# A hybrid SSM and attention layer: the row of reciprocal softmax sums is stored by one transfer from ScalarE's queue, and put in order by its load

## The chip, the cores and the metric

The kernel runs on one core of a Trainium2 chip. The metric is device time in microseconds, the median of several runs; beside it stands one execution taken by the hardware profiler, from which all durations and waits come. The engines are TensorE (PE, with its weight loads PEld), VectorE (DVE), ScalarE (ACT), GpSimd (POOL) and SyncE (SP), which here only issues transfers. Transfers are issued by SyncE, ScalarE and GpSimd, each from its own in-order queue, and carried by 16 DMA engines.

## The reference, cut to what matters

The layer normalises x, multiplies it by one wide matrix, and feeds two branches, a Mamba-2 scan and a forgetting attention, that are gated, merged, multiplied by an output matrix and added to x. The change lies in the attention. There are 16 heads of 64 channels, a sequence of 1024, and queries in 8 blocks of 128:

```
s = einsum(q, k) * scale + fcum[query] - fcum[key]
s = where(key <= query, s, -inf)
prob = softmax(s)
o = einsum(prob, v)
y_att = o * silu(z_att)
```

All numbers are float32. Where precision needs it, an operand is split in a high and a low part.

## The kernel before

**Stages.** The projections are matrix products by a seven-product scheme on halves of the operands (classes `Pair` and `Plain`), 12 matrix multiplications of 128x512 for each product. They form one long stream (`Stream`), and everything else is done beside it: first the scan (to about 600 us), then attention (about 660 to 1146 us), then the rest of the branch and output products. Attention calls `fill`, which lets the stream run for so many half products between two pieces of attention, and so gives TensorE work while VectorE and ScalarE deal with the scores. The operands of the later branch products (tiles x0 to x6, an h and an l part each) are loaded and split during the second half of attention, from about 930 us on.

**Attention.** The loop at L1666 goes over 8 pairs of heads (hp), and for each over six groups g of two query blocks against half of the keys. In a step, `scores` makes the products q k in a PSUM bank s (4 such banks, also used for pt and tp below). VectorE adds the forget bias fb and takes the extreme (L1526, tile nm), ScalarE takes the exponential and its sum (L1530, tile sm). `turned` transposes the result with TensorE (pt), and copies it out (p, L1548 on VectorE, L1550 on ScalarE). `weighted` multiplies by v into a bank av.

**The row of reciprocal sums.** After every second group, three times for a pair of heads (n = 0, 1, 2), the sums are brought together (`settle`, `scale`), which gives a tile ns of 128 queries x 8 columns: two parts h, two heads e of the pair, two query blocks t. The output has channels on the partitions and queries along the row, so the values must lie along a row, the same on all 64 partitions of a head. `send` turns ns with TensorE (tp), ScalarE copies the 8x128 result to st (L1452), and GpSimd stores it with two transfers (L1454) to st_dram, with the order changed so that a head's 512 values follow each other. `take` loads that row for each head e by SyncE to 64 partitions of rb (L1460). VectorE multiplies av by the gate (`free`, L1479), and later by rb (`out`, L1491 for n < 2, L1485 for n = 2). The first pair's three rows are stored near 689, 711 and 730 us, and the last pair's last one near 1136 us: 24 rows in all.

**What sets the order.** A scheduler orders each engine's instructions, except that TensorE's, and all that are wrapped in `pin`, keep the order of the program. The two stores L1454 are pinned. GpSimd does little else in attention: differences of operands (L214, L1587, L1593, L1607) and their stores (L196), stores of outputs (ya_dram, L1581) and of gated branch products (ms_dram, L1102). ScalarE's queue issues the stores of gates gs and ga (L654), 256 KB each, right behind the tanh that makes them (L653). ScalarE also makes the high parts of weights (wop, L354), copies of PSUM (s, L410 and L418) and of operands (L278, L281). SyncE issues all loads and some stores, in order: while it waits for a store to land before a load, the loads behind it wait too. Transfers from SyncE and ScalarE share eight semaphores, used in turn; one that takes a semaphore waits until the earlier transfer on it has landed.

Of the kernel before, what the change touches and what calls it, by code (L numbers as in the profile page):

```python
# [8 lines left out]
F32 = mybir.dt.float32  # L9
# [7 lines left out]
P = 128  # L17
T = 1024
D = 1024
NK = D // P  # L20
KH = NK // 2
NT = T // P
HALF = 512
# [63 lines left out]
def hybrid_layer(ctx: ExitStack, tc, a, out):  # L87

    nc = tc.nc
# [17 lines left out]
    nc.vector.memset(eps4, 4.0 * EPS)  # L107

    f_dram = tc.dram_tile([HEADS, T], F32, name="f_dram")
    st_dram = tc.dram_tile([NK, 3, 2, HALF], F32, name="st_dram")  # L110
    r_dram = tc.dram_tile([NG, T], F32, name="r_dram")
    rr_dram = tc.dram_tile([NG, T], F32, name="rr_dram")
    cs_dram = tc.dram_tile([HEADS, T], F32, name="cs_dram")
# [18 lines left out]
    def turn(out_, in_, idn=ident):  # L132
        return tc.keep_in_program_order(nc.tensor.transpose(out_, in_, idn))  # L133

    def pin(op):
        return tc.keep_in_program_order(op)

    def small(name="th"):
        return gp.tile([P, HALF], F32, tag="th", name=name)
# [1053 lines left out]
    with tc.tile_pool(name="pro", bufs=1, reuse_waits="tile", side="right") as pro, tc.tile_pool(  # L1193
        name="prop", bufs=1, space=PSUM, reuse_waits="tile", side="right"
# [116 lines left out]
    with tc.tile_pool(name="ssm", bufs=1, reuse_waits="tile", side="right") as sp, tc.tile_pool(  # L1311
        name="ssmp", bufs=1, space=PSUM, reuse_waits="tile", side="right"
# [42 lines left out]
    with tc.tile_pool(name="att", bufs=1, reuse_waits="tile", side="right") as ap, tc.tile_pool(  # L1355
        name="attp", bufs=1, space=PSUM, reuse_waits="tile", side="right"
    ) as pp:
        rows = [slice(64 * e, 64 * e + 64) for e in range(2)]
# [42 lines left out]
        class Heads:  # L1401
# [44 lines left out]
            def send(self, n):  # L1446

                tp = pp.tile([P, HALF], F32, tag="s", bufs=4, name="tp")
                turn(tp[0:8, 0:P], self.ns[n].rearrange("p h e t -> p (h e t)"))
                st = small("st")[0:8, 0:P]  # L1450
                with tc.high_priority():
                    nc.scalar.activation(st, tp[0:8, 0:P], AF.Copy)  # L1452
                for h in range(2):
                    pin(nc.gpsimd.dma_start(st_dram[self.hp, n, :, 256 * h : 256 * h + 256], st[4 * h : 4 * h + 4, :]))  # L1454

            def take(self, n):

                rb = self.rb[n] = small("rb")
                for e in range(2):
                    nc.sync.dma_start(rb[rows[e], :], st_dram[self.hp, n, e : e + 1, :].to_broadcast([64, HALF]))  # L1460

            def load_gates(self, n):

# [300 lines left out]
```

## Time and profile before

| what | value |
|---|---|
| runs (us) | 1291.77, 1297.5, 1297.4 |
| median (us) | 1297.4 |
| profiled execution, its time (us) | 1294.79 |
| profiled execution, its span (us) | 1293.1 |
| mean granted TensorE clock | 0.997 |
| instructions | 21078 |
| HBM traffic over the span | 182 GB/s |
| stores L1454 | 48, 2 KB each |
| loads L1460 | 48, 128 KB each |

The span is the time from the first to the last instruction of the program in the profiled execution; its time as a run is 1.7 us more. In the rows, a tile's buffer numbers are left out, L12 is line 12 of the kernel, SPq and ACTq are the queues' own instructions (an issue of a transfer, a wait), and "out<-in" names what is written and read. A wait is put down to the last of the things waited for. The time from issue to landing is given by tile and source line, for those transfers whose landing the trace shows.

### The profile page before, as it was taken

Reading aid. Unit: us, or ns where it says so; the run is one execution under the profiler, and the core shown is the slowest. Engines: PE = TensorE matmul, PEld = TensorE weight load, DVE = VectorE, ACT = ScalarE, POOL = GpSimd, SP = SyncE. Lnnn points to the kernel's source line nnn. Section 1 sums busy time; section 2 is a strip of 40 time slices with the busy share of each in tenths; the row PEclk is TensorE's granted clock in tenths of the full one; section 3 lists DMA queues with packets and bytes.
Section 4 is the critical chain, followed back from the end, with each engine's and each line's share of the span. In section 5 each row is a group of like instructions: output and inputs, shape, how many; then the busy total and the mean of one; then the engine's idle time right before and its main releaser. Section 6 shows DMA issues by size and latency. Waiting matters only on the chain. (4 is left out here: it accounts for less than half of the span.)

```text
span 1293.1 us, 21078 instructions
## 1 busy us (share of the span) xinstructions
PE 1253.8 (97%) x7066; PEld 986.1 (76%) x7066; DVE 1014.7 (78%) x1979; ACT 794.3 (61%) x1728; POOL 284.6 (22%) x307
## 2 busy tenths in 40 slices
PE   6999999999999999899999999999999999999998
PEld 4787888788888888688776777777767777678786
DVE  6998888888789878788676766676789767876875
ACT  8755666466556756566555666566677556743654
POOL 0000330024102320143001222222121313256052
PEclk9999999999999999999999999999999999999999
DMA  7332543644363545445564657666677657665932
GB/s 281 104 106 71 154 148 121 199 140 146 127 210 116 153 153 164 122 154 154 168 237 153 221 175 224 193 208 196 228 282 250 219 178 253 230 219 189 364 112 102
DMA packets 154669, 233.60 MB, mean 181 GB/s; under 512 B 17216, under 2 KB 62656, under 8 KB 154560
## 3 DMA queue, kind: packets, MB, share of 16 engines
q1 hardware_dynamic: 142016, 205.53, 49.8%
q0 software_dynamic: 6400, 16.10, 3.3%
q10 hardware_dynamic: 6144, 10.62, 2.2%
q8 instruction: 56, 0.92, 0.3%
q14 instruction: 53, 0.43, 0.1%
HBM read 162.99 MB, written 72.34 MB: 182 GB/s over the span
## 5 line engine op out<-in xcount | busy, mean ns | idle before, releaser
L356 DVE TENSOR_TENSOR wop<-sum,wop 128x512 fp32r<-128x512 f32 x174 | 140.5, 808 | 53.4 <-ACT wop L354 52.7
L354 ACT ACTIVATE wop<-sum 128x512 fp32r<-128x512 f32 x174 | 108.8, 626 | 99.0 <-DVE sum L363 44.7
L1530 ACT ACTIVATE ex<-ex,nm 128x512 f32<-128x512 f32 (+1 forms) x192 | 116.1, 606 | 76.9 <-DVE nm L1526 75.7
L410 ACT ACTIVATE s<-pb 128x512 f32<-128x512 f32 x141 | 83.5, 592 | 97.3 <-PE pb L130 95.9
L130 PE MATMUL pc<-x3h,wop 128*128 128x512 f32 x384 | 131.6, 399 | 2.5 <-ACT wop L354 2.0
L130 PE MATMUL pb<-x0h,wop 128*128 128x512 f32 x384 | 132.2, 400 | 0.7 <-ACT x0h L1246 0.6
L130 PE MATMUL pc<-x2h,wop 128*128 128x512 f32 x384 | 131.4, 399 | 0.4 <-DVE u L422 0.4
L130 PE MATMUL pb<-x6h,wop 128*128 128x512 f32 x376 | 129.2, 399 | 1.6 <-ACT s L410 1.6
L130 PE MATMUL pb<-x5h,wop 128*128 128x512 f32 x376 | 128.3, 398 | 1.3 <-ACT s L410 1.3
L130 PE MATMUL pb<-x4h,wop 128*128 128x512 f32 x376 | 128.6, 398 | 0.2 <-DVE wop L356 0.2
L356 DVE TENSOR_TENSOR wop<-raw,wop 128x512 fp32r<-128x512 f32 x149 | 104.3, 702 | 29.8 <-ACT wop L354 29.5
L1526 DVE CUSTOM_DVE_ANT_0 ex<-s,fb 128x512 f32<-128x512 f32 (+1 forms) x192 | 96.8, 553 | 24.4 <-PE s L130 24.3
L354 ACT ACTIVATE wop<-raw 128x512 fp32r<-128x512 f32 x151 | 93.8, 623 | 15.8 <-PE pc L130 10.1
L130 PE MATMUL pd<-x1h,wop 128*128 128x512 f32 x264 | 89.1, 396 | 0.0
L130 PEld LDWEIGHTS pc<-x3h,wop 128*128 128x128 f32 x384 | 72.1, 188 | 20.2 <-issue 3.8
L130 PEld LDWEIGHTS pb<-x0h,wop 128*128 128x128 f32 x384 | 72.5, 189 | 17.2 <-ACT x0h L1246 1.3
L130 PEld LDWEIGHTS pc<-x2h,wop 128*128 128x128 f32 x384 | 72.1, 188 | 16.1 <-DVE u L422 0.8
L130 PEld LDWEIGHTS pb<-x6h,wop 128*128 128x128 f32 x376 | 70.6, 188 | 18.1 <-ACT s L410 2.7
L130 PEld LDWEIGHTS pb<-x5h,wop 128*128 128x128 f32 x376 | 70.6, 188 | 17.5 <-ACT s L410 2.2
L130 PEld LDWEIGHTS pb<-x4h,wop 128*128 128x128 f32 x376 | 70.5, 188 | 15.7 <-issue 0.7
L130 PE MATMUL s<-k,q 64*128 64x512 f32 (+3 forms) x576 | 75.7, 373 | 6.2 <-DVE p L1548 4.4
L214 POOL TENSOR_TENSOR wd<-wd 128x256 f32<-128x256 f32 x32 | 31.3, 978 | 228.3 <-DMA wd<-in_wo 125.7
(341 smaller groups left out, 3012.1 us busy)
## 6 DMA issues: line engine op xcount, KB each, us to landing
raw<-in_wu SPq DMA_DIRECT2D x128, 256.0 KB, 3.7
csb<-cs_dram SPq DMA_DIRECT2D x32, 256.0 KB, 5.5
fb<-f_dram SPq DMA_DIRECT2D x16, 512.0 KB, 6.5
rb<-st_dram SPq DMA_DIRECT2D x48, 128.0 KB, 3.2
wd<-in_wo SPq DMA_DIRECT2D x40, 128.0 KB, 3.1
xt<-in_x SPq DMA_DIRECT2D x8, 512.0 KB, 5.8
gs_dram<-th ACTq DMA_DIRECT2D x16, 256.0 KB, 3.4
qh_dram<-th SPq DMA_DIRECT2D x16, 256.0 KB, 5.2
```

The costliest lines, as they stand in the source:

```text
L130: return tc.keep_in_program_order(nc.tensor.matmul(*args, **kw))
L214: pin(nc.gpsimd.tensor_tensor(t[out_], t[a_], t[b_], ALU.subtract))
L354: nc.scalar.activation(op[:, 0], src, AF.Copy, scale=sign)
L356: nc.vector.tensor_tensor(op[:, 1], src, op[:, 0], ALU.subtract)
L410: nc.scalar.activation(s, ps, AF.Copy)
L1526: nc.vector.tensor_tensor_reduce(o, s[e][:, 0:w], fb[hp, h][:, e, 0:w], 1.0, 3.0e38, ALU.add, ALU.min, nm)
L1530: pin(nc.scalar.activation(o, o, AF.Exp, scale=-1.0, bias=nm, accum_out=hd.at(hd.sm, i, h, e)))
```

## The change

The row's place in DRAM keeps the order in which TensorE turned it: 8 rows (h, e, t) of 128 values. ScalarE's queue stores all of it with one transfer of 4 KB (8 rows of 512 bytes), not pinned, and GpSimd's two stores are gone. The load now puts the pieces in order: for a head e, each of the 64 partitions takes two pieces of 256 values (1 KB), one for each h, where it took one of 512 (2 KB). The number of loads and their bytes are the same.

```diff
-    st_dram = tc.dram_tile([NK, 3, 2, HALF], F32, name="st_dram")
+    st_dram = tc.dram_tile([NK, 3, 8, P], F32, name="st_dram")
...
                 with tc.high_priority():
                     nc.scalar.activation(st, tp[0:8, 0:P], AF.Copy)
-                for h in range(2):
-                    pin(nc.gpsimd.dma_start(st_dram[self.hp, n, :, 256 * h : 256 * h + 256], st[4 * h : 4 * h + 4, :]))
+                    nc.scalar.dma_start(st_dram[self.hp, n], st)
...
                 rb = self.rb[n] = small("rb")
+                by_head = st_dram[self.hp, n].rearrange("(h e t) c -> e h (t c)", h=2, e=2)
                 for e in range(2):
-                    nc.sync.dma_start(rb[rows[e], :], st_dram[self.hp, n, e : e + 1, :].to_broadcast([64, HALF]))
+                    to = rb[rows[e], :].rearrange("p (h c) -> p h c", h=2)
+                    nc.sync.dma_start(to, by_head[e : e + 1].to_broadcast([64, 2, 256]))
```

The store's line is L1453 after the change, the load's L1461, and lines from there on are one more than before.

On ScalarE, at the first row of attention (hp = 0, n = 0), the order before is this:

```order
L1530 ACTIVATE ex,sm<-ex,nm 128x256 x2
L1530 ACTIVATE ex,sm<-ex,nm 128x128 x2
L1452 ACTIVATE st<-tp 8x128
L410 ACTIVATE s<-pb 128x512
L354 ACTIVATE wop<-sum 128x512
L1550 ACTIVATE p<-pt 128x512
```

And this is the same place of ScalarE after it:

```order
L1531 ACTIVATE ex,sm<-ex,nm 128x256 x2
L1531 ACTIVATE ex,sm<-ex,nm 128x128 x2
L1452 ACTIVATE st<-tp 8x128
L1453 DMA st_dram<-st 8x128
L410 ACTIVATE s<-pb 128x512
L354 ACTIVATE wop<-sum 128x512
L1551 ACTIVATE p<-pt 128x512
```

The store stands directly behind the copy, ahead of an eviction of the stream (L410). At 9 of the 24 rows, the scheduler put one or two other activations between copy and store.

On GpSimd, at the same place, before (t_s and x, th are differences of operands and their store, ya_dram takes the outputs of attention):

```order
L214 TENSOR_TENSOR x<-x,th 128x512
L1454 DMA st_dram<-st 2x2x128 x2
L196 DMA t_s<-x 128x512
L214 TENSOR_TENSOR x<-th,x 128x512
L196 DMA t_s<-x 128x512
L1454 DMA st_dram<-st 2x2x128 x2
```

And after:

```order
L214 TENSOR_TENSOR x<-x,th 128x512
L196 DMA t_s<-x 128x512
L214 TENSOR_TENSOR x<-th,x 128x512
L196 DMA t_s<-x 128x512
L214 TENSOR_TENSOR th<-x,th 128x512
```

The store of a difference no longer stands behind two stores of a row, which wait for ScalarE's copy. SyncE's loads and TensorE's order at this place are the same as before; TensorE's is the same throughout.

On ScalarE after the change, at the first row of the sixth pair (hp = 5, n = 0), where the operands x1 to x6 are made; here each row names in brackets the semaphores that it waits for:

```order
L1452 ACTIVATE st<-tp 8x128 [waits DMAHW6_49,PE_49]
L1453 DMA st_dram<-st 8x128 [waits DMAHW3_49,Activation_49]
L281 ACTIVATE x6h<-x6l 128x512 [waits DMAHW1_49]
L281 ACTIVATE x6h<-x6l 128x512
L410 ACTIVATE s<-pb 128x512 [waits PE_49]
```

The store waits for the copy (Activation_49), and for the earlier transfer on its own semaphore (DMAHW3_49), which at this place is SyncE's last load of x2l. Before, the copy stood directly ahead of the two L281, with no wait between.

## The prediction

> **What bounds the kernel now.** I began with the page: its first part says that TensorE is the engine to shorten for, and that nothing else helps unless TensorE stands still less.
>
> ```profile
> PE 1253.8 (97%) x7066; PEld 986.1 (76%) x7066; DVE 1014.7 (78%) x1979; ACT 794.3 (61%) x1728; POOL 284.6 (22%) x307
> ```
>
> The change touches the attention stage alone, from 680 to 1146 us. The busy times by window (columns: window, length, then busy us and instructions of PE, PEld, DVE, ACT, POOL, then granted clock, DMA share, GB/s) show where TensorE is short of work there.
>
> ```profile
> 540.00:550.00 10.00, 7.49 (x36) 5.76 (x34) 9.61 (x17) 7.24 (x17) 1.90 (x2) 1.00 0.50 125
> 700.00:710.00 10.00, 6.79 (x47) 4.67 (x47) 7.79 (x23) 5.13 (x12) 0.00 (x0) 0.83 0.32 114
> 720.00:920.00 200.00, 198.90 (x1344) 151.82 (x1342) 138.90 (x348) 126.54 (x314) 47.80 (x62) 1.00 0.65 208
> 920.00:1010.00 90.00, 86.64 (x585) 64.96 (x587) 73.94 (x178) 65.58 (x162) 13.87 (x20) 1.00 0.72 247
> 1010.00:1080.00 70.00, 70.00 (x492) 53.33 (x491) 52.70 (x135) 39.90 (x106) 19.19 (x28) 1.00 0.66 220
> 1080.00:1146.00 66.00, 61.86 (x391) 46.21 (x390) 54.48 (x125) 46.04 (x108) 17.70 (x22) 1.00 0.68 229
> 1146.00:1293.00 147.00, 139.89 (x614) 114.51 (x612) 105.65 (x154) 72.38 (x145) 62.87 (x44) 0.99 0.57 195
> ```
>
> TensorE stands 3.2 us in 700 to 710, and only there is its clock below full: 0.83 over 10 us is 1.7 us more lost. From 720 to 920 it stands 1.1 us in 200. From 920 to 1010 and from 1080 to 1146 it stands 3.4 and 4.1 us, with VectorE 82% busy in both. Then the waits of the stage (who waited for whom: us in total, times, longest), since the row goes by the store L1454 and the loads L1460 to VectorE's L1491 and L1485.
>
> ```profile
> POOL st_dram L1454 <- ACT st L1452: 163.5, 24, 17.4
> ...
> DVE o L1491 <- DMA rb<-st_dram: 11.7, 8, 4.4
> ...
> DVE zr L1485 <- DMA rb<-st_dram: 3.1, 3, 1.8
> ```
>
> GpSimd's 163.5 us are idle time of an engine that is 22% busy, and worth nothing by themselves. VectorE's 14.8 us are the most that an earlier row can give back. SyncE's queue waits too, with every load that stands behind:
>
> ```profile
> SPq L1460 <- DMA st_dram<-st: 87.6, 21, 7.3
> ```
>
> The longest of VectorE's waits is that of the first row of all. Here it is engine by engine in the timeline (start, length, what; in brackets the idle time before it): ScalarE, GpSimd, SyncE's queue, VectorE, TensorE.
>
> ```profile
> 688.81 0.25 ACT L1452 ACTIVATE st<-tp 8x128 f32<-8x128 f32 x1
> 690.44 0.60 ACT L410 ACTIVATE s<-pb 128x512 f32<-128x512 f32 x1 [1.39 <-PE pb L130]
> ```
> ```profile
> 689.36 1.30 POOL L1454 DMA_DIRECT2D st_dram<-st  x2 [7.59 <-ACT st L1452]
> ```
> ```profile
> 688.46 0.41 SPq L1395 DMA_DIRECT2D fb<-f_dram  x1
> 696.28 1.13 SPq L1460 DMA_DIRECT2D rb<-st_dram  x2
> ```
> ```profile
> 700.55 0.69 DVE L1491 TENSOR_TENSOR o<-o,rb 128x512 f32<-128x512 f32 x1 [4.37 <-DMA rb<-st_dram]
> ```
> ```profile
> 705.52 1.65 PE L130 MATMUL s<-k,q 64*128 64x512 f32 x6 [3.21 <-DVE p L1548]
> ```
>
> The copy ends at 689.06, the two stores are out at 690.66, the queue holds the loads until 696.28, VectorE gets the row at 700.55 after 4.37 us of waiting. The eviction L1548, which comes later on VectorE, is late with it, and TensorE stands 3.21 us for the bank.
>
> **The change part by part.** *The first row, the one with a visible price.* GpSimd's issues (0.30 us behind the copy, then 1.30) give way to one on ScalarE's queue. The store's landing has two kinds of rows: the old store, and the stores of gates that ScalarE's queue issues already.
>
> ```profile
> L1454 POOL DMA_DIRECT2D st_dram<-st x48: 549/577/736, 689.4 to 1136.6; - x48
> ...
> DMA to landing us min/median/max: 1.6/3.0/6.3
> ```
> ```profile
> L654 ACTq DMA_DIRECT2D gs_dram<-th x16: 326/327/354, 38.6 to 829.0; - x16
> ...
> DMA to landing us min/median/max: 2.0/3.7/6.6
> ```
>
> The gates' rows are 256 KB against 4 KB here, so their 3.7 is on the safe side, and I take it: 689.06 + 0.33 + 3.7 = 693.1 for the loads' issue instead of 696.28. Their landing, KB and us by the list of transfers:
>
> ```profile
> fb<-f_dram SPq DMA_DIRECT2D x16, 512.0 KB, 6.5
> rb<-st_dram SPq DMA_DIRECT2D x48, 128.0 KB, 3.2
> ...
> q<-qh_dram SPq DMA_DIRECT2D x32, 128.0 KB, 3.7
> ```
>
> The loads now come in pieces of 1 KB, as the q loads do, so 3.7 for 3.2. The forget bias (fb, 512 KB) ahead of them on the queue should have landed at 688.46 + 6.5 = 695.0, inside that time. The second load goes out 0.5 us behind the first: 693.1 + 0.5 + 3.7 = 697.3, against 700.55. That is 3.2 of VectorE's 4.37 us, and as much as TensorE stood. With the stall goes the half clock: a stall of 2.51 us elsewhere left the clock of its window at 1.00 (540 to 550 above).
>
> ```profile
> 543.54 0.33 PE L133 MATMUL tr<-ident,xs 128*128 128x128 f32 x1 [2.51 <-DVE xs L811]
> ```
>
> So the term is at most 3.2 + 1.7 = 4.9 us. If the store lands as late as the latest gate (6.6), the loads go out at 696.0, 0.3 us earlier than now, and lose 0.5 to the smaller pieces: +0.2. I take **-4.5**, near the upper end, since the median landing gives it, less 0.4 for what is late next (the score bank also waits for ScalarE's copies of pt).
>
> The Trainium skill (TensorE: Matmul & The Clock Gate, Part 1) says that the clock is halved after an idle window of about 3.4 us that runs free of the kernel. By that rule a stall of 3.21 us halves it in some runs only, and in those without it the term would be -2.8; no run here shows which they are.
>
> *The other rows.* 14.8 - 4.4 = 10.4 us of VectorE's waits remain, the longest 1.8. From 720 to 920 TensorE stands 1.1 us in all, so there they are covered by its own work. In the two windows where it stands 7.5 us together, VectorE is near its limit and a wait could pass through. I take **-1.0**; the ends are 0 and -4 (about half of that standing, and well under the 10.4 us).
>
> *ScalarE's issues.* 24 more on an engine that runs in order. What one costs directly behind its producer, in a gate's rows:
>
> ```profile
> 747.36 0.62 ACT L653 ACTIVATE th<-th 128x512 f32<-128x512 f32 x1
> 748.01 0.33 ACTq L654 DMA_DIRECT2D gs_dram<-th  x1
> 748.38 0.51 ACT L1530 ACTIVATE ex<-ex,nm 128x256 f32<-128x256 f32 x1 [0.40 <-ACT th L653]
> ```
>
> 0.40 us each, 9.6 for all. Where ScalarE idles anyway it is hidden (after the first copy it idles 1.39 us, until 690.44), and where the order sets other work between copy and store it overlaps. Queued behind it are evictions L410 and weight parts L354, for which TensorE waits. I take **+0.5**; the ends are 0 and +9.6, the upper one far since TensorE stands 8.6 us in all windows from 720 to 1146, whatever the cause.
>
> *A wait that comes with it.* Transfers from SyncE and ScalarE signal on the same eight semaphores in turn, and one that reuses a semaphore waits for the earlier transfer. For the copy that ends at 983.56 this is the last load of x2l:
>
> ```profile
> L266 SPq DMA_DIRECT2D x2l<-ys_dram x4: 319/348/498, 975.2 to 977.9; - x4
> ...
> DMA to landing us min/median/max: 7.3/7.3/7.4
> ```
> ```profile
> 983.31 0.25 ACT L1452 ACTIVATE st<-tp 8x128 f32<-8x128 f32 x1
> 983.47 1.14 ACT L281 ACTIVATE x6h<-x6l 128x512 fp32r<-128x512 f32 x2
> ```
>
> It lands at 977.9 + 7.3 = 985.2, so ScalarE, which goes on at once now, would stand 1.6 us there, and the eviction L410 behind it. I take **+1.0**, with ends 0 and +1.6.
>
> *What has one answer.* The stores taken from GpSimd free 48 x 0.58 = 28 us of an engine nobody waits for here: 0. SyncE's queue gets most of its 87.6 us back, and the q, v and ys loads behind go out earlier; neither TensorE nor VectorE waits for these: 0. TensorE's order is unchanged; VectorE's and ScalarE's is shuffled in places after 940, unpriced, 1 us either way.
>
> The sum is -4.5 - 1.0 + 0.5 + 1.0 = **-4.0 us**. The profiled execution took 1294.79 us (span 1293.1 and 1.7 around it), so its like would take 1290.8. The median of the three runs is 1297.4, 2.6 above the profiled one; against that median my forecast is **1293.4**. About 0.5% (6.5 us) is what a measurement of this kernel can tell from no change, so this is within it.
>
> **The rivals.** *The store lands no sooner (chance 0.25).* The 16 DMA engines carry fb and the weights when it comes, whoever issued it. Only the issue time is saved: 0.30 + 0.58, less 0.5 for the smaller pieces, so 0.4 us at the first row, the clock still falls, and nothing comes from the others. With +0.5 and +1.0 this is +1.1: 1298.5. For it speaks that ScalarE's landings (2.0/3.7/6.6) are not shorter than GpSimd's (1.6/3.0/6.3); against it, that a row of 4 KB is compared with gates of 256 KB. The Trainium skill (DMA: Bandwidth & Descriptors, section "Issuing engines are not separate DMA queues") says just this: another issuing engine saves only the sequencer's time.
>
> *VectorE's waits reach TensorE (0.22).* In the two tight windows VectorE at 82% sets the pace, and every row that comes earlier counts: -4.9 for the first and -4.0 for the others, +0.5 for the issues, no semaphore wait: -8.4, 1289.0. For it speaks the 7.5 us that TensorE stands there; against it, that the longest wait there is 1.8 us and the windows hold few of them.
>
> *Slower: ScalarE stands at its stores (0.09).* From 940 on transfers land late, and the semaphore of each store is held by a load, as at 983. With ten stores from 940 to 1136, 1.6 us each and all of it passed on through L410, this is +16 beside the -4.5: +11.5, 1308.9. It decides from more than 1.1 us per store on (11 us, over the 4.5 gained and the 6.5 that can be told). For it speaks that ScalarE is in order and 73% busy from 920 to 1010; against it, that gates on the same queue do without such waits now: ScalarE's bracketed 0.40 us at 748 is the issue alone.
>
> **How the numbers follow.** The forecast has 0.44. Its own range is from +0.2 + 1.6 to -4.9 - 4: by its terms 1288 to 1299 (the issues' far end of +9.6 is left to the slower rival). The first rival lies in it, the second at 1289 with its ends below. For the 2.6 us between profile and median I add that much at the lower side of the second rival, 1286, and 1.5 at the upper, 1300; only the slower rival and a remnant lie outside. Faster by over 0.5% (below 1290.9) are most of the second rival and the lower edge of the forecast: 0.20 + 0.09 = 0.29. Slower (above 1303.9) is the third rival nearly alone: 0.08. The rest, 0.63, is within 0.5%.
>
> **What would show it.** In the profile after: the load of the first row is issued near 693 instead of 696.28, VectorE's wait before its first product with rb is near 1 us, TensorE's 3.21 us near 705 are gone and the window 700 to 710 has clock 1.00. VectorE's waits for rb sum to 5 us or less, the queue's for the store to half of 87.6. ScalarE stands once, near 983, for 1 to 2 us. I am wrong if the row lands as late as before (first rival), if the window's clock stays at 0.83, if TensorE's standing from 920 to 1146 changes by more than 3 us, or if ScalarE shows idle time ahead of many stores.

## The result and the profile after

| | before | after |
|---|---|---|
| median of 22 runs each (us) | 1295.16 | 1298.67 |
| lowest to highest (us) | 1291.77 to 1298.44 | 1294.58 to 1304.21 |
| profiled execution, its time and span (us) | 1294.79, 1293.1 | 1299.44, 1297.4 |
| its mean granted clock | 0.997 | 0.994 |

The ratio is 1.0028 (95% interval 1.0017 to 1.0039): 3.6 us slower. That is within the 0.5% that I called no change, but on the other side of before than the 4.0 us faster that I forecast. The 1298.67 lies inside my range (1288 to 1299) by luck: before's own median came out 2.2 us lower than the 1297.4 from which I counted. As a difference, +3.6 lies above the +1.8 that was my upper end.

The engines' busy times first, from the page of after: TensorE is busy 3 us more than before (1253.8), and GpSimd 30 us less (284.6).

```profile
PE 1256.8 (97%) x7066; PEld 988.2 (76%) x7066; DVE 1018.5 (78%) x1979; ACT 794.3 (61%) x1728; POOL 254.7 (20%) x259
```

The windows of after, with the boundaries and columns of the prediction (PE, PEld, DVE, ACT, POOL, granted clock, DMA share, GB/s):

```profile
540.00:550.00 10.00, 7.24 (x29) 5.57 (x27) 9.53 (x17) 6.97 (x17) 1.42 (x2) 0.83 0.49 119
700.00:710.00 10.00, 8.43 (x67) 6.14 (x66) 8.96 (x24) 5.92 (x15) 1.88 (x2) 1.00 0.39 138
720.00:920.00 200.00, 199.27 (x1364) 152.42 (x1364) 140.68 (x349) 127.87 (x318) 35.88 (x42) 1.00 0.64 205
920.00:1010.00 90.00, 84.03 (x534) 62.28 (x531) 69.98 (x171) 62.73 (x154) 8.08 (x10) 0.96 0.72 243
1010.00:1080.00 70.00, 70.00 (x496) 53.41 (x496) 51.52 (x131) 38.54 (x100) 15.06 (x21) 1.00 0.66 214
1080.00:1146.00 66.00, 61.51 (x388) 45.51 (x385) 54.75 (x128) 46.77 (x114) 11.52 (x14) 0.97 0.69 231
```

700 to 710 went half of the way that I forecast: TensorE stands 1.6 us instead of 3.2, at full clock, where I had it not standing at all. But from 920 to 1010 it stands 6.0 us instead of 3.4, and the clock is 0.96 over 90 us, about 3.5 us more lost; from 1080 to 1146 the clock is 0.97. (At 540 to 550, ahead of everything that the change touches, a stall of 2.76 us halved the clock in this execution, where 2.51 us did not in before's: chance, for which the last section has the reason.)

The waits of after that belong to the change (us in total, times, longest):

```profile
DVE o L1492 <- DMA rb<-st_dram: 4.6, 4, 2.1
ACT x6h L281 <- DMA x2l<-ys_dram: 2.7, 1, 2.7
SPq L1461 <- DMA st_dram<-st: 67.6, 20, 5.4
```

VectorE's waits for the row (L1492 here; L1486 has none left) fell from 14.8 to 4.6 us, as I said. SyncE's queue waits 67.6 us instead of 87.6; I had expected half. The middle line is new. Here is the place in after's timeline, ScalarE and then TensorE:

```profile
981.15 0.25 ACT L1452 ACTIVATE st<-tp 8x128 f32<-8x128 f32 x1
983.79 0.29 ACTq L1453 DMA_DIRECT2D st_dram<-st  x1
984.13 1.15 ACT L281 ACTIVATE x6h<-x6l 128x512 fp32r<-128x512 f32 x2 [2.73 <-DMA x2l<-ys_dram]
985.19 0.58 ACT L410 ACTIVATE s<-pb 128x512 f32<-128x512 f32 x1
...
988.27 0.58 ACT L1551 ACTIVATE p<-pt 128x512 f32<-128x512 f32 x1
```
```profile
988.90 1.65 PE L130 MATMUL s<-k,q 64*128 64x512 f32 x5 [1.92 <-ACT p L1551]
```

The copy of row (5,0) ends at 981.40; its store goes out 2.4 us later, when the load of x2l has landed that signals on the same semaphore. Everything behind it on ScalarE is 2.8 us late, down to the copy p (L1551), which starts 7.1 us behind the copy of the row and in before 4.3; and for p TensorE stands 1.92 us. The four loads of x2l had gone out from 972.5 to 974.7:

```profile
L266 SPq DMA_DIRECT2D x2l<-ys_dram x4: 320/460/627, 972.5 to 974.7; - x4
```

Of the other 23 stores, 22 go out within 0.1 us of their copy; the one left, of row (7,1), has a section below. (5,0) is also the only row at which the earlier transfer on the store's semaphore was still under way when the copy ended. The rows of all stores in after, with those of the loads:

```profile
L1461 SPq DMA_DIRECT2D rb<-st_dram x48: 579/594/1866, 695.7 to 1139.8; - x48
...
L1453 ACTq DMA_DIRECT2D st_dram<-st x24: 269/292/524, 690.8 to 1137.9; - x24
```

A store costs ScalarE 0.29 us, a load in two pieces costs SyncE's queue 0.59 us where the load in one took 0.45.

### The profile page after: what moved, and what is told of

The parts are those of the page before. It is cut to its first block, busy times and chain, and to the rows that moved or that the text cites. A ratio compares the mean times of both kernels' runs of the same rounds, so it can differ in the third digit from the quotient of the medians.

```text
span 1297.4 us, 20977 instructions
## 1 busy us (share of the span) xinstructions
PE 1256.8 (97%) x7066; PEld 988.2 (76%) x7066; DVE 1018.5 (78%) x1979; ACT 794.3 (61%) x1728; POOL 254.7 (20%) x259
## 5 line engine op out<-in xcount | busy, mean ns | idle before, releaser
L356 DVE TENSOR_TENSOR wop<-sum,wop 128x512 fp32r<-128x512 f32 x174 | 135.6, 780 | 57.7 <-ACT wop L354 56.7
L410 ACT ACTIVATE s<-pb 128x512 f32<-128x512 f32 x141 | 83.5, 592 | 103.1 <-PE pb L130 102.0
L130 PE MATMUL pb<-x0l,wop 128*128 128x512 f32 x192 | 75.9, 395 | 0.5 <-DVE x0l L1248 0.5
```

The source lines that it names most:

```text
L130: return tc.keep_in_program_order(nc.tensor.matmul(*args, **kw))
L356: nc.vector.tensor_tensor(op[:, 1], src, op[:, 0], ALU.subtract)
L410: nc.scalar.activation(s, ps, AF.Copy)
```

## The experiments

After the result I had these theories. A: the stand at (5,0) makes the loss, 2.4 us of it directly and the rest by the half clock behind it. B: the pieces of 1 KB, or loads that go out earlier, make it. C: the scheduler's other order of ScalarE and VectorE after 940 makes it. Later came D to H, named in the expectations. Each kernel was timed beside before on one chip; "us" in the table is the ratio's distance from 1 times before's median of about 1294. "At half clock" is the mean over a kernel's runs of (1 - mean granted clock) times span, which is the most that TensorE can have lost so; for before it is 3.3 to 4.3 us in the four groups. In every trace, 1.7 to 3.6 us of it lie in the last microseconds of the execution. (The 3.5 of e2 leaves out one run of ordinary time whose clock reads 0.948.) Kernels of different groups (e1 to e5, e6 to e9, e10 to e13, e14 to e17, each on its own chip) are compared by their ratios to before; the difference between two kernels is known to about 0.2%, 2.5 us.

| kernel | ratio to before, 95% interval | us | at half clock |
|---|---|---|---|
| after | 1.0028, 1.0017 to 1.0039 | +3.6 | 7.8 |
| after again (e13) | 1.0046, 1.0024 to 1.0068 | +6.0 | 7.8 |
| e1 all rows: one GpSimd store | 0.9981, 0.9968 to 0.9994 | -2.5 | 2.9 |
| e17 the same again | 0.9987, 0.9973 to 1.0000 | -1.7 | 3.1 |
| e2 ScalarE for pairs 0 to 3 | 0.9982, 0.9967 to 0.9997 | -2.3 | 3.5 |
| e3 ScalarE for pairs 4 to 7 | 1.0025, 1.0010 to 1.0041 | +3.2 | 6.5 |
| e5 after, (5,0) and (7,1) on GpSimd | 0.9981, 0.9967 to 0.9995 | -2.5 | 3.9 |
| e6 after, (5,0) on GpSimd | 1.0019, 1.0002 to 1.0036 | +2.5 | 6.4 |
| e12 after, (7,1) on GpSimd | 1.0032, 1.0020 to 1.0045 | +4.1 | 7.3 |
| e7 e1 with (5,0) on ScalarE | 0.9996, 0.9981 to 1.0011 | -0.5 | 3.8 |
| e8 after, both rows on SyncE | 1.0002, 0.9986 to 1.0018 | +0.3 | 4.7 |
| e9 pieces, two GpSimd stores | 1.0006, 0.9988 to 1.0023 | +0.8 | 3.9 |
| e15 the same again | 1.0006, 0.9993 to 1.0020 | +0.8 | 3.7 |
| e14 e9 with row (0,0) on ScalarE | 0.9994, 0.9982 to 1.0007 | -0.8 | 4.0 |
| e10 e6 with before's order at (7,1) | 0.9991, 0.9978 to 1.0005 | -1.2 | 4.4 |
| e11 e5 with after's order at (7,1) | 1.0012, 0.9998 to 1.0026 | +1.6 | 5.9 |
| e16 e1 with fb's load behind the row's | 0.9963, 0.9947 to 0.9979 | -4.8 | 2.7 |

**Which half of the rows costs (e1, e2, e3, e5).** The edits choose the engine of the store; where GpSimd stores, it does so with one transfer, in before's place.

```diff
# e1
-                    nc.scalar.dma_start(st_dram[self.hp, n], st)
+                    pin(nc.gpsimd.dma_start(st_dram[self.hp, n], st))
# e2; e3 has self.hp >= 4; e5 has (self.hp, n) not in ((5, 0), (7, 1))
+                    if self.hp < 4:
+                        nc.scalar.dma_start(st_dram[self.hp, n], st)
+                    else:
+                        pin(nc.gpsimd.dma_start(st_dram[self.hp, n], st))
```

> All 24 rows are stored by one transfer of GpSimd (in before's place), the turned layout and the loads in two pieces stay. Theory A (the late loss comes from ScalarE standing at its store of the row (5,0), 2.4 us, for a load of x2l that landed late): no store is on ScalarE, so nothing is lost at 986 to 995; the first row gains little, one issue of 0.58 instead of two (1.30): -1 us against before, between -2.5 and +0.5. Rival B (the pieces of 1 KB, or loads behind them that go out earlier, cost the time): +3 to +4, as in after. Rival C (ScalarE's and VectorE's changed order after 940, which the added store brings): like A here, -1.

> ScalarE stores the rows of the first four pairs (12 rows), GpSimd with one transfer those of the last four; ScalarE's and VectorE's order after 940 is then that of before but for two moved rows. Theory A: the first row's gain of about 3 us stays, the stand of 2.4 us and its half clock go: -3 us against before, between -1.5 and -4.5, and no idle time of ScalarE ahead of a store. Rival B (pieces, earlier loads): +3 to +4. Rival C (changed order after 940): -3 as by A, since that order is undone too.

> The opposite half: GpSimd stores the rows of the first four pairs, ScalarE those of the last four. Each engine's order but for the stores is that of after. Theory A: ScalarE stands 2 to 3 us at the store of row (5,0), TensorE loses about 5 us at 985 to 995 and 1 to 2 more after 1120, the first row gains about 1: +4 to +6 us against before, more than after's +3.6. Rival B: +3 to +4, as after. Rival C: +4 to +6 too.

> As after, but the two rows at which ScalarE stood in after's profile, (5,0) and (7,1), are stored by GpSimd; 22 rows stay on ScalarE, and nearly all of after's order of ScalarE and VectorE stays with them. Theory A: the loss at 986 to 995 goes, the first row's gain stays: -2.5 us against before, between -1 and -4. Rival B and rival C: +2 to +4, as after, since pieces and order are after's.

Measured: -2.5, -2.3, +3.2, -2.5 (e3 a little under what theory A had). B falls: e1, e2 and e5 have the pieces and the earlier loads and are faster than before. ScalarE's issues themselves cost nothing that shows: none (e1), 12 (e2) and 22 of them (e5) give the same time. The loss hangs on two rows, (5,0) and (7,1). C falls but for these two places, since e5 keeps the rest of after's order. That e1 gains as much as e2 was a miss: I had thought that the gain needed ScalarE.

**Which of the two rows (e6, e7, e8, e9).** e6 is after with (5,0) alone on GpSimd, and apart from one row on VectorE every engine keeps after's order. e7 is e1 with (5,0) alone on ScalarE. e8 is after with both rows stored from SyncE. e9 has the turned layout and the pieces, but two GpSimd stores.

```diff
# e6: ScalarE if (self.hp, n) != (5, 0), else GpSimd; e7: if (self.hp, n) == (5, 0)
# e8: ScalarE if (self.hp, n) not in ((5, 0), (7, 1)), else
+                        nc.sync.dma_start(st_dram[self.hp, n], st)
# e9
-                    nc.scalar.dma_start(st_dram[self.hp, n], st)
+                for h in range(2):
+                    pin(nc.gpsimd.dma_start(st_dram[self.hp, n, 4 * h : 4 * h + 4], st[4 * h : 4 * h + 4, :]))
```

> After with the one row (5,0) stored by GpSimd; TensorE, ScalarE, GpSimd and SyncE keep after's order word for word, and VectorE's has one row moved. Theory A: the loss at 986 to 995 is that store's stand alone, so it goes (about 5 us); the 0.9 us stand at (7,1) stays and may cost 1 to 2: -1.5 us against before, between -3 and 0. Rival B (pieces, earlier loads) and rival C (changed order): +3 to +4, as after.

> The reverse: GpSimd's single store for 23 rows (the first of these kernels took 2.5 us off before), and ScalarE stores row (5,0) alone. Theory A: ScalarE stands 1.5 to 2.5 us there, TensorE stalls 1.5 to 2 us more about 990 and its clock is halved behind it in most runs: +2 us against before, between +0.5 and +4, which is 3 to 6 more than with all rows on GpSimd. Rival B or C: -2.5, as with all rows on GpSimd.

> After with the rows (5,0) and (7,1) stored from SyncE's queue, where they wait for the same earlier transfer of x2l on the same semaphore, so that these rows land as late as in after, but SyncE's queue stands instead of ScalarE. Theory A (it is ScalarE's stand that costs): as with these rows on GpSimd, -2.5 us against before, between -4 and -0.5. Rival D (the late row itself, or the loads behind it, cost the time): +2 to +4.

> The turned layout and the loads in two pieces of 1 KB, with two stores by GpSimd as before. If the 2.5 us that one GpSimd store takes off before come from the second store's issue (0.58 us less until the row is out, at each row): 0 to +1 us against before, the load's longer issue (0.59 for 0.45 us) being the price. If they come from the load in pieces: -2 to -3.

Measured: +2.5, -0.5, +0.3, +0.8. e6 is a clear miss for A: without the stand at (5,0) most of the loss stays. e7 and e8 miss too: with the stand alone, e7 is 1.2 to 2.0 us over e17 and e1, where I had 3 to 6, and that can't be told from nothing; e8 lies between what A and D had. That the stand is real and costs TensorE time, the windows around it show, first after's:

```profile
980.00:997.00 17.00, 14.56 (x63) 10.22 (x62) 11.42 (x30) 9.04 (x23) 0.54 (x1) 0.80 0.75 262
```

Then those of e6, with the same order and no store there:

```profile
980.00:997.00 17.00, 16.51 (x105) 11.99 (x104) 15.90 (x39) 12.53 (x32) 1.07 (x2) 1.00 0.90 316
```

In e6 TensorE stands 0.5 us in these 17 us, in after 2.4, and there at a clock of 0.80 beside. (e6 comes to this row 5.2 us later than after, so the two windows don't hold quite the same work: a stall of 1.07 us at 998.70 belongs to e6's place too. The table below compares the same work.) e8 shows whose wait it is. SyncE's queue there issues the store 2.0 us after the copy, and ScalarE goes on at once:

```profile
983.74 0.29 SPq L1456 DMA_DIRECT2D st_dram<-st  x1
```
```profile
981.50 0.25 ACT L1452 ACTIVATE st<-tp 8x128 f32<-8x128 f32 x1
981.66 1.14 ACT L281 ACTIVATE x6h<-x6l 128x512 fp32r<-128x512 f32 x2
```

So the wait belongs to the transfer (the semaphore it takes), and the queue that issues it is the one that stands. What e8 loses against e5 (2.7 us) is not resolved: the intervals overlap.

To see where TensorE loses time, I took each matrix multiplication's start in a trace and subtracted the start of the same one in before's. The change of that lateness over four stretches (before's times, us; each from one profiled execution):

| kernel | 560 to 712, first row | 985 to 997, (5,0) | 997 to 1122 | 1122 to 1145, (7,1) |
|---|---|---|---|---|
| after | -3.2 | +5.6 | -1.7 | +2.6 |
| after again (e13) | -0.6 | +2.9 | -2.9 | +0.6 |
| e3 | -3.1 | +5.3 | -3.0 | +0.5 |
| e12, (5,0) on ScalarE | -0.9 | +5.4 | -2.4 | 0.0 |
| e7, (5,0) on ScalarE | -3.4 | +3.5 | -2.8 | -0.3 |
| e6, (5,0) on GpSimd | -0.8 | +0.8 | -3.0 | +0.6 |
| e5, both on GpSimd | -0.1 | +1.6 | -2.8 | +0.1 |
| e1 | -0.9 | 0.0 | -1.8 | +0.1 |

The stand costs 2.9 to 5.6 us where ScalarE stores (5,0), of which after's changed order alone, in e5 and e6, makes 0.8 to 1.6. Much of it is given back by 1122: TensorE stands 2.5 us in that stretch in before (1.1, 0.5, 0.4 and 0.5 of it at 1002, 1096, 1111 and 1116), 1.4 in after and 0.5 to 0.6 in the next six kernels of the table. Lateness is not the whole reason, since e1, which is not late, gains 1.8 there too. And something else costs at (7,1).

**The place at (7,1) (e10, e11, e12).** In after's profile the store of (7,1) also goes out late, 0.87 us after its copy, and I had read it as a second wait for a semaphore. ScalarE's timeline says otherwise:

```profile
1122.15 0.25 ACT L1452 ACTIVATE st<-tp 8x128 f32<-8x128 f32 x1
1123.16 0.62 ACT L1531 ACTIVATE ex<-ex,nm 128x384 f32<-128x384 f32 x1 [0.76 <-DVE nm L1527]
1123.27 0.27 ACTq L1453 DMA_DIRECT2D st_dram<-st  x1
```

The store stands behind an exponential that waits for VectorE. But with the store in its list, the scheduler set the instructions around it in another order. ScalarE's, before and after:

```
before: ex, x5h, x5h, ex (128x384) ... x2h, x5h, x2h, x3h, x2h, wop, p, st
after:  ex, store, ex (128x384), x5h, x5h ... x2h, x2h, wop, x5h, x2h, x3h, p, st, store
```

The split x3h, for which TensorE waits, has moved behind a split of x2 and a weight part. e10 and e11 separate order and store by edges that only order ScalarE's issue, without a wait (`earlier` and `later` are the instructions named in the expectations). e12 is after with (7,1) alone on GpSimd, e13 is after itself.

```diff
+        tc.add_manual_dep(later, earlier.name, mybir.DependencyInfo(
+            mybir.DependencyClass.NoSync, mybir.DependencyReason.DATA), reason="order")
```

> Row (5,0) on GpSimd, all others on ScalarE, the store at (7,1) among them; but at (7,1) ScalarE's other instructions are held in before's order (the second exponential of 128x384 behind the two splits of x5, the split of x2 and the weight part behind the split of x3h), which the added store had changed. Theory E (at (7,1) it is the changed order that costs, not the store): -2.5 us against before, between -4 and -0.5, as with both rows on GpSimd. Theory A (the store at (7,1) itself): +2.5, as with row (5,0) alone on GpSimd.

> The reverse: rows (5,0) and (7,1) on GpSimd, but ScalarE's instructions around (7,1) held in after's order. Theory E: +2.5 us against before, between +0.5 and +4, though no store is there. Theory A: -2.5, as with both rows on GpSimd and before's order.

> After with the row (7,1) alone stored by GpSimd, which brings back before's order there; the stand at (5,0) stays. By the runs so far, row (5,0) costs about 2 to 3 us: 0 us against before, between -1.5 and +2. If (5,0) costs all of it (my first reading of after's profile): +3.5.

> After itself, beside the other three on one chip, for the comparison: +3.6 us against before, between +2 and +5, and about 3.5 us more lost at half clock than before (mean granted clock 0.994 over its runs).

Measured: -1.2, +1.6, +4.1, +6.0. e5, e6, e10 and e11 differ at (7,1) alone, and make two pairs each way. With the store on the same engine and the order changed (ScalarE's, and with it a few rows of VectorE's and one pair of SyncE's loads), e11 is 0.31% (4.0 us) over e5, and e6 0.28% (3.6 us) over e10. With the order the same and the store on ScalarE, e10 is 0.10% over e5 and e6 0.07% over e11, which can't be told from nothing. So at (7,1) it is the order, as a whole. TensorE's waits in e11, which has no store of ScalarE there:

```profile
1126.14 0.55 PE L130 MATMUL s<-k,q 64*128 64x128 f32 x5 [1.26 <-DVE p L1552]
1134.11 0.49 PE L130 MATMUL pc<-x3h,wop 128*128 128x512 f32 x1 [1.20 <-ACT x3h L281]
1135.09 0.49 PE L130 MATMUL pc<-x3l,wop 128*128 128x512 f32 x1 [0.48 <-DVE x3l L282]
```

And the same place in e10:

```profile
1132.94 0.50 PE L130 MATMUL pc<-x3l,wop 128*128 128x512 f32 x1 [0.72 <-DVE x3l L282]
```

1.68 us of standing close together against 0.72 (the wait of 1.26 for p at 1126 has one of 1.16 at 1121 in e10 as its like). The difference in time, 3.6 to 4.0 us, is larger than that. In the column "at half clock", e11 has 2.0 us more than e5, and e6 2.0 more than e10, so a part of it may be half clock. Where the runs lose it, the profiles don't show: the two stands for x3 are there in all five with after's order (after, e13, e3, e6, e11), and only in after's own does the clock fall behind them, at 1138:

```profile
1137.29 0.51 PE L130 MATMUL pc<-x3h,wop 128*128 128x512 f32 x1 [1.15 <-ACT x3h L281]
1138.26 0.67 PE L130 MATMUL pc<-x3l,wop 128*128 128x512 f32 x1 [0.46 <-DVE x3l L282]
```

The rest of the price stays open.

e12 was a miss: the order at (7,1) is before's again, and its +4.1 lies between the two results of after (+3.6, and +6.0 in e13, which is above the +5 that I had allowed). Either of the two places alone, (7,1) in e6 or (5,0) in e12, brings most of the loss, and both together (after) not the sum. So the two places together are worth about 6 us (after against e5), but neither has a price of its own that holds in every kernel: (5,0) makes 6.6 us between e5 and e12, and 2.0 or less between e1 and e7. Why, I can't settle from one profile each.

**The first row (e14 to e17).** The largest term of the forecast was still unpriced. e14 is e9 with row (0,0) alone stored by ScalarE; every other instruction of every engine stays where it was. e15 is e9 and e17 is e1, each again as a base. e16 is e1 with one ordering edge, on SyncE's queue: fb's load (L1395) behind the first row's two loads.

```diff
# e14, ahead of e9's loop of two stores
+                if (self.hp, n) == (0, 0):
+                    with tc.high_priority():
+                        nc.scalar.dma_start(st_dram[self.hp, n], st)
+                    return
# e16: the same helper as in e10, with later = fb's load, earlier = the second load of rb
```

> Only the first row (0,0) is stored by ScalarE with one transfer; the other 23 keep GpSimd's two stores, the layout is turned and the loads are in pieces. Each engine's order is that of the kernel with the pieces alone, run beside it. My forecast's first term (the row of ScalarE lands 3.2 us earlier and takes TensorE's stall and the half clock with it): -4.5 us against the pieces alone. Theory F (the store lands 5 to 6 us after its copy from either queue, so that only 1 us is saved): 0 to -1.5, and VectorE's wait for the row stays over 1.5 us.

> The kernel with the pieces alone (two stores by GpSimd for all rows) again, as the base of the first-row run beside it: 0 to +1 us against before, as in its first run (+0.06%).

> All rows by one GpSimd store, and SyncE's load of the forget bias fb (512 KB), which goes out ahead of the first row's two loads, is put behind them; nothing else moves. Theory G (the first row's store is late because the 16 DMA engines carry fb, weights and differences when it comes): the store lands 1 to 1.7 us earlier, VectorE waits 1.5 to 2.5 us for the row instead of 3.6, TensorE's clock is halved behind it less often: 1 to 2 us faster than without the move, -0.3% against before. Theory H (the landing does not depend on fb): as without the move, -0.2%.

> All 24 rows by one GpSimd store, again, as the base of the run with the bias moved and to see whether its gain holds: -2.5 us against before, between -1 and -4.

Measured: -0.8, +0.8, -4.8, -1.7. e14 against e15 is 0.12%, or 1.6 us, with nothing inside the interval and 4.5 us outside: theory F, and not my term. VectorE still waits for the row in e14:

```profile
701.22 0.69 DVE L1497 TENSOR_TENSOR o<-o,rb 128x512 f32<-128x512 f32 x1 [2.84 <-DMA rb<-st_dram]
```

e16 shows what the row had been waiting for. In e17, without the move, the store goes out at 690.04, and the loads, which wait for its landing, 5.6 us later:

```profile
690.04 0.70 POOL L1453 DMA_DIRECT2D st_dram<-st  x1 [7.91 <-ACT st L1452]
```
```profile
689.16 0.43 SPq L1395 DMA_DIRECT2D fb<-f_dram  x1
695.62 1.27 SPq L1461 DMA_DIRECT2D rb<-st_dram  x2
```
```profile
699.23 0.69 DVE L1492 TENSOR_TENSOR o<-o,rb 128x512 f32<-128x512 f32 x1 [2.38 <-DMA rb<-st_dram]
```

In e16, with fb's 512 KB out of its way, 3.6 us later, from the same GpSimd:

```profile
688.71 0.70 POOL L1453 DMA_DIRECT2D st_dram<-st  x1 [7.87 <-ACT st L1452]
```
```profile
692.27 1.26 SPq L1461 DMA_DIRECT2D rb<-st_dram  x2
693.62 0.73 SPq L1395 DMA_DIRECT2D fb<-f_dram  x1
```
```profile
696.25 0.69 DVE L1492 TENSOR_TENSOR o<-o,rb 128x512 f32<-128x512 f32 x1 [0.72 <-DMA rb<-st_dram]
```

TensorE does not stand at all there in e16 (22.00 us busy of 22):

```profile
690.00:712.00 22.00, 22.00 (x144) 16.91 (x143) 17.27 (x42) 15.05 (x36) 4.45 (x5) 1.00 0.54 169
```

e16 is the fastest of all kernels here: 0.37% (0.21 to 0.53%) under before. Against e17, beside it on the same chip, that is 3.1 us, just clear of the noise, where I had 1 to 2. Theory G holds: in e17 the store landed at 695.57, right behind fb (695.40), in e16 at 692.22, before fb was issued.

## Why the prediction was wrong, point by point

**The first row, -4.5: the term that failed first.** I took the store's landing from the gates' rows (3.7 us, "on the safe side") and put the loads at 693.1, 4.0 us behind the copy; in after they go out at 695.7. Over the ten traces in which ScalarE stores this row, the loads go out 5.0 to 6.2 us behind the copy, 5.6 on average; with two GpSimd stores it is 6.6 to 7.2 in three traces. So 1.3 us are saved, not 3.2. The Trainium skill (DMA: Bandwidth & Descriptors, "Issuing engines are not separate DMA queues") says that transfers run on the same 16 DMA engines whichever engine starts them, and that issuing on several engines saves only the sequencers' time; from the copy's end to the last store being out it was 1.6 us in before and is 0.55 in after, which is 1.05 of the 1.3, so the runs agree. My first rival said so too, and had 0.25; that its 1298.5 is so near the measured 1298.67 is luck, since it meant +1.1 and had no loss at either of the two places. I set fb's landing (695.0) beside the store's and took it to be inside my time; in truth fb was what the store waited for (e16). The upper end of the term, 4.9 us, is near what e16 takes off at this place in the profile, 4.5 us; but e17, where TensorE still stands 1.2 us for the row, takes off 4.0 as well, because its clock doesn't fall.

The size of the term was also a matter of which execution was profiled. TensorE's stall at this row is 1.2 to 3.4 us over the 17 traces in which fb goes out first, and the clock falls behind it in 9 of them; before's profile had 3.21 us and the fall. e9 and e15, which store this row as before does, have 2.2 and 2.4 us, and the fall in e15 alone; e13, the same kernel as after, has 2.9 us and the fall, where after has 1.6 and none.

**The wait at (5,0), +1.0 with ends 0 and +1.6: right in its place, too small.** ScalarE stood 2.4 us instead of 1.6 (1.5 to 2.4 in the five profiles with this store). After's TensorE ran 2.0 us ahead of before here, and the copy came 2.2 us earlier than the row of before from which I reckoned; the last load of x2l went out 3.2 us earlier (974.7 for 977.9), but took 9.0 us to land instead of 7.3, so that it landed only 1.5 us earlier (983.7 for 985.2). And I let it end at ScalarE. TensorE lost 2.9 to 5.6 us there in the profiles: a stall of 1.9 us for p (two of 1.4 and 1.0 in e7), and the half clock behind it in three of the five traces.

**The changed order, "unpriced, 1 us either way".** This is the second step that failed. At (7,1) alone it is worth 3.6 to 4.0 us where (5,0) is on GpSimd (e6 against e10, e11 against e5), and near 985 another 0.8 to 1.6 in the profiles. I had looked at the order for what the store moved, and not at what stood ahead of an operand that TensorE waits for: x3h, a wait of 1.1 to 1.2 us in all five traces with the new order, and in none of the others.

**ScalarE's issues, +0.5.** Right; with 0, 12 and 22 of them the time is the same within about 2 us. **The other rows, -1.0.** VectorE's waits fell as forecast; what they are worth by themselves no run separates. (The longest that I left for these rows, 1.8, was misread: before has one of 2.51 us at 875.6, in the stretch where TensorE hardly stands.) **What had one answer, 0.** Wrong in one point: the pieces cost nothing that can be told (e9 and e15, +0.8 us with 0 in the interval; in e9 they land in 3.2 us, as before's loads do, where I had taken 3.7), but taking away GpSimd's second issue, with a few rows of the other engines that the scheduler moved for it, is worth 2.5 to 3.2 us (e17 against e15, e1 against e9), just clear of the noise, which I had counted at the first row alone, inside the 3.2. At which rows it comes about I didn't find in single traces.

**The slower rival (0.09)** named the right mechanism at (5,0) and the wrong extent: one store stood, not ten, and it cost through the copy p and the clock rather than through L410. The sum of the change, as the runs have it: -2 to -3 from the shorter issue and the earlier rows, +6 from the two places on ScalarE (after against e5: 6.1 us). The time lost at half clock went up by as much as the slowdown, 7.8 us in after's runs against 3.3 to 4.3 in before's of the other groups (for the 22 runs of before beside after's, no clock is known); how much of the 6 us it makes at each place is not shown.

## What to carry to other kernels

Before a transfer is put on an engine that also computes, look up which earlier transfer its semaphore belongs to, and read in the trace when that one lands: an in-order engine stands until then. When a scheduler orders the work, compare its whole list before and after, above all what now stands ahead of an operand that the bounding engine waits for. And when a small row lands late, look at the large transfer issued just ahead of it before changing who issues the row: moving one 512 KB load behind it gave 3.1 us (e16 against e17), and the change of engine lost 3.6.

## What the runs showed of the hardware that I had not expected

**The clock is judged in fixed windows of 3.41 us, and about half an idle window is enough.** In every one of the 18 traces, all falls of the clock lie on one grid of 3.41 us (in after, 544.5, 988.2 and 1138.4 are 0, 130 and 174 steps apart). Two windows of after, and in each case the one behind it:

```profile
984.84:988.25 3.41, 1.62 (x8) 0.68 (x7) 3.41 (x7) 3.41 (x7) 0.00 (x0) 1.00 0.68 262
988.25:995.07 6.82, 6.17 (x20) 4.09 (x21) 6.77 (x18) 3.34 (x9) 0.54 (x1) 0.50 0.70 228
1135.03:1138.43 3.40, 1.79 (x9) 0.96 (x8) 3.06 (x6) 3.05 (x8) 0.54 (x1) 1.00 0.64 242
1138.44:1141.84 3.40, 3.40 (x13) 1.86 (x14) 1.93 (x4) 2.07 (x4) 0.00 (x0) 0.50 0.19 63
```

And the stall of 2.53 us at the first row in e2, which lay across a boundary:

```profile
701.57:704.97 3.40, 2.01 (x12) 1.42 (x10) 3.33 (x9) 2.92 (x7) 0.80 (x1) 1.00 0.22 83
704.99:708.38 3.39, 2.27 (x26) 1.56 (x28) 2.81 (x6) 0.79 (x2) 0.99 (x2) 1.00 0.38 151
708.40:711.80 3.40, 3.40 (x24) 2.40 (x21) 1.79 (x7) 2.84 (x10) 0.00 (x0) 1.00 0.23 78
```

1.4 and 1.1 us idle, and the clock stays. Over the 18 traces, the first 20 us and the last few left out: of 21 windows with 1.95 us idle or more, all were followed by half clock; of 24 with 1.6 to 1.95, 10; of some 6600 with less, 4, three of which were at half clock already. The Trainium skill (TensorE: Matmul & The Clock Gate, Part 1) speaks of an idle window of about 3.4 us that runs free of the kernel; the length and the free phase agree, but the window need not be idle, about half of it suffices here. (To the letter, that rule would never halve the clock for the 3.21 us of before's first row, which fill no whole window; the prediction's "in some runs only" doesn't follow from it. The window that they lay in, 702.1 to 705.5, was followed by half clock.) So two stalls of 1.2 and 0.5 us in one window cost up to 1.7 us more in after and nothing more in e11, one of 2.5 may cost nothing more, and which it is can change from run to run.

**A store of 4 KB took 5.5 us from issue to landing behind a load of 512 KB on another queue, and 3.5 us without it** (e17, e16; one profile each), though the two share no queue.
